# One address residue modulo 512 bytes for the operands of the split products

## The chip, the cores and the metric

The kernel runs on one core of one Trainium2 chip. The metric is the device time of one execution in microseconds. Inputs, weights and the output lie in the chip's memory, and everything is float32.

The engines are named as the profile names them: PE is TensorE's matrix multiplication, PEld its load of the stationary operand, DVE is VectorE, ACT is ScalarE, POOL is GpSimd, SP is SyncE, which issues most transfers.

## The reference

One encoder block over 1024 tokens of width 1024: a normalisation, one wide input projection, three mixers side by side (dilated window attention, grouped attention with normalised queries and keys, cross attention into 256 memory tokens), a gate on each, a projection of each, a merge by sigmoid gates, an output projection and a residual.

```python
h = rms_norm(x, g_pre[layer])
a_qkv, bq, bk, bv, mq, ga, gb, gm, mg = jnp.split(h @ w_in[layer], split_at, axis=-1)
...
ya = (oa * jax.nn.silu(ga)) @ w_br_a[layer]
yb = (ob * jax.nn.silu(gb)) @ w_br_b[layer]
ym = (om * jax.nn.silu(gm)) @ w_br_m[layer]
gates = jax.nn.sigmoid((mg + b_merge[layer]).astype(jnp.float32)).astype(dt).reshape(b, s, N_BRANCHES, d)
merged = gates[:, :, 0] * ya + gates[:, :, 1] * yb + gates[:, :, 2] * ym
out = merged @ w_out[layer]
x = x + rms_norm(out, g_post[layer])
```

## The kernel before

**Split products.** PE multiplies in a reduced format, `float32r`. To keep the precision of float32, an operand is split into a high part, rounded by a copy on ACT, and a low part, the rest, by a subtraction on DVE (`split`, lines 89 to 91). A product is then three matmuls into one PSUM bank: high by high, high by low and low by high. Each matmul loads its stationary operand (128 by 128, so 512 bytes of each partition) and streams its moving operand, 512 columns (2048 bytes of each partition) or 256 columns. In a row of the profile such as `s<-hh,vS` the first name behind the arrow is the moving operand, the second the stationary one.

**Stages**, by the line of their matmuls, in order of time:

- L354: keys and values of the grouped attention, 256 columns moving (`wbh`, `wbl`), stationary the tokens `hh`, `hl` (the split of the normalised input, eight tiles each, for the whole kernel).
- L525: keys and values of the memory, 256 columns, moving `mh`, `ml`, stationary `wh`, `wl`.
- L284, L286, L288: queries of the grouped attention, 256 columns, moving `wbh`, `wbl`, stationary `hh`, `hl`; woven with it the memory attention, whose products are L110 (`passes`), 256 columns, with `kmh`, `kml`, `mqh`, `mql`, `vmh`, `vml`, `mph`, `mpl`.
- L128, L130, L132 (`dense`): gate units, 512 columns, moving `hh`, `hl`, stationary `wh`, `wl`; woven with the grouped attention: L772 (row minima), L790 and L791 (scores), L806 (values, in float32).
- L1221 and L1272: values of the dilated attention by seven products of blocks (Strassen's scheme), 512 and 256 columns, stationary the tokens (`hh`, `hl`, and sums of tokens in `aq`, `ak`, `kT`, `vA`), moving the weights (`wh`, `wl`, `sl`).
- L1311 (`pair_product`): queries, keys, one gate and the merge gates, 25 pairs of units, again by seven products of blocks, 2100 matmuls of 512 columns. The stationary operand is a block of weights, in `wh`, `wl` or in the tiles `vS10` to `vS21`; the moving one a block of tokens, in `hh`, `hl`, `aq`, `ak`, or in `vA` and `kT` tiles.
- L1899: the merge projections, 512 columns, moving `hh`, `hl` or `bh`, `bl`, woven with the dilated attention (L1570, L1584, L1618, L1640, L1650, L1660, all float32).
- L2041: the last merge projections. L2123: the output projection by seven products of blocks, moving `wB`, `wT` tiles, stationary `hh`, `hl`, `aq`, `ak`, `wh`, `wl`.

**What sets the order.** PE's instructions stand in the order in which the program writes them; in some stages the other engines' do too, and a scheduler places the rest. Tiles come from pools. Pools on the left of the partition's memory are stacked from low addresses upward, pools on the right from the top downward, and a pool's tiles lie one behind the other, so each tile's address follows from the sizes of all that were laid before it. The left stack begins with the constants (`cs`, then `ones`, `mhalf`, `rb`, `rcol`, `nrcol`, `rsq`, `hbm`, each rounded up to 32 bytes), followed by `hh` and `hl`, the weight tiles `wr`, `wh`, `wl`, and the pools of each stage. `cs` is the table of constants that one transfer brings: 426 columns, of which 128 and 129 are unused, and 146 to 169 hold the biases of the merge gates. `ones` is a column of ones, and `hbm` half of those biases.

Of the kernel before, what the change touches and what calls it, by code (L numbers as in the profile page):

```python
# [8 lines left out]
F32 = mybir.dt.float32  # L9
R = mybir.dt.float32r  # L10
AF = mybir.ActivationFunctionType
OP = mybir.AluOpType
# [5 lines left out]
P = 128  # L18
# [4 lines left out]
C_ID, C_GP, C_GM, C_BM, C_END = 0, 130, 138, 146, 426  # L23
# [10 lines left out]
def block(ctx: ExitStack, tc: tile.TileContext, x, xT, memT, cst, msk, bcst, tabA, gpost,  # L34
          wu, wv, wb, wmem, wbr, wout, out):
    nc = tc.nc
    V, A, G, PE = nc.vector, nc.scalar, nc.gpsimd, nc.tensor

    const = ctx.enter_context(tc.tile_pool(name="const", bufs=1))
# [23 lines left out]
    def pss1():  # L63
        return bank["p"].tile([P, 512], F32, name="s1", tag="s1", bufs=bank["n"][1])

    def pst():
        bank["i"] += 1
        return bank["p"].tile([P, 4, 128], F32, name="tr", tag="t", bufs=bank["n"][2])

    def pso():  # L70
        return bank["p"].tile([P, 512], F32, name="ov", tag="o", bufs=bank["n"][3])
# [3 lines left out]
    cs = const.tile([P, C_END], F32, name="cs")  # L75
    nc.sync.dma_start(cs, cst)
    ident = cs[:, C_ID:C_ID + 128]
    ones = const.tile([P, 1], F32, name="ones")
    V.memset(ones, 1.0)
    mhalf = const.tile([P, 16], F32, name="mhalf")  # L80
    V.memset(mhalf, -0.5)
# [1 line left out]
    rcol = const.tile([P, NT], F32, name="rcol")  # L83
    nrcol = const.tile([P, NT], F32, name="nrcol")
    rsq = const.tile([P, NT], F32, name="rsq")
    hbm = const.tile([P, 24], F32, name="hbm")
    V.tensor_scalar(hbm, cs[:, C_BM:C_BM + 24], 0.5, None, op0=OP.mult)

    def split(dst_h, dst_l, src):
        A.activation(dst_h, src, AF.Copy)  # L90
        V.tensor_tensor(dst_l, src, dst_h.bitcast(F32), op=OP.subtract)  # L91
# [15 lines left out]
    def passes(out_ps, terms):  # L107
        n = len(terms)
        for i, (a, b) in enumerate(terms):
            PE.matmul(out_ps, a, b, start=i == 0, stop=i == n - 1)  # L110
# [107 lines left out]
    def pool(name, side="left"):  # L218
        p = tc.tile_pool(name=name, bufs=1, side=side, reuse_waits="tile")
        return p, p.__enter__()  # L220
# [7 lines left out]
    mbp, mb = pool("mb", "right")  # L228
# [37 lines left out]
    def fetch_wb(c0):  # L266
        raws = []
        for i in range(2):
            raw = wp.tile([P, 1024], F32, name="wr", bufs=WR)
            raws.append(raw.rearrange("p (k f) -> p k f", k=4))  # L270
        return raws, mb.tile([P, 8, 256], R, name="wbh"), mb.tile([P, 8, 256], R, name="wbl")
# [162 lines left out]

    PROJ = 8 * 24 * 109.0
    raws, *wkv = fetch_wb(512)

    def load_wkv(i):
        nc.sync.dma_start(raws[i // 2][:, i % 2 * 2:i % 2 * 2 + 2], wb[:, 2 * i:2 * i + 2, 512:768])
# [114 lines left out]
    mtp, mt_ = pool("mt")  # L554
    fp["p"] = mt_

    def m_att(h):
        qh, ql = MQ[h]
        for _ in range(4):
            yield 250  # L560
        st = {}

        def scores(n):
            sv = pss1().rearrange("p (t k) -> p t k", t=2)
            nm = mt_.tile([P, 2], F32, name="mnm", bufs=3)
            l = mt_.tile([P, 2], F32, name="mls", bufs=3)
            pm = mt_.tile([P, 2, 256], F32, name="pm", bufs=2)
            for j in range(2):
                t = slice((2 * n + j) * 128, (2 * n + j) * 128 + 128)
                passes(sv[:, j], [(qh[:, t], kmh[:, h]), (qh[:, t], kml[:, h]), (ql[:, t], kmh[:, h])])  # L570
            V.tensor_reduce(nm, sv, axis=AX.X, op=OP.min)
            V.tensor_tensor(nm, nm, rcol[:, 2 * n:2 * n + 2], op=OP.mult)
            for j in range(2):
                A.activation(pm[:, j], sv[:, j], AF.Exp, scale=nrcol[:, 2 * n + j:2 * n + j + 1], bias=nm[:, j:j + 1],
                             accum_out=l[:, j:j + 1])
            rl = mt_.tile([P, 2], F32, name="mrl", bufs=4)
            V.reciprocal(rl, l)
            for j in range(2):
                fp["mv"] = V.tensor_scalar(pm[:, j], pm[:, j], rl[:, j:j + 1], None, op0=OP.mult)
            st[n] = pm  # L580

        def trans(n):
            pm = st[n]
            tp = pst().rearrange("p (k t) q -> p k t q", k=2)
            for kt in range(2):
                for j in range(2):
                    PE.transpose(tp[:, kt, j, :], pm[:, j, kt * 128:kt * 128 + 128], ident)
            ph = mt_.tile([P, 2, 256], R, name="mph", bufs=2)
            pl = mt_.tile([P, 2, 256], R, name="mpl", bufs=2)
            split(ph, pl, tp.rearrange("p k t q -> p k (t q)"))  # L590
            st[n] = (ph, pl)

        def pv(n):
            ph, pl = st.pop(n)
            o = pso()
            terms = []
            for kt in range(2):
                terms += [(vmh[:, kt, h], ph[:, kt]), (vmh[:, kt, h], pl[:, kt]), (vml[:, kt, h], ph[:, kt])]
            passes(o[:, 0:256], terms)
            om = mt_.tile([P, 256], F32, name="om", bufs=2)  # L600
            A.activation(om, o[:, 0:256], AF.Copy)
            nc.sync.dma_start(od[2, h, :, n * 256:n * 256 + 256], om)

        for n in range(7):
            if n < 4:
                scores(n)
            yield 654
            if 0 <= n - 2 < 4:
                trans(n - 2)
            yield 436  # L610
            if 0 <= n - 3 < 4:
                pv(n - 3)
            yield 654
# [46 lines left out]
    early[len(queue)] = lambda: load_w(wu[U_G + 11])  # L660
    weave(1)
    weave(2, m_att(0), M_COST, 1.2)
    weave(2, m_att(1), M_COST, 1.2)
    weave(1, m_att(2), M_COST, 1.0)
    weave(1, m_att(3), M_COST, 1.0)
    while pend:
# [813 lines left out]
    with ExitStack():  # L1480
# [224 lines left out]
        def plan(it, pre, nxt):  # L1705
# [7 lines left out]
            def tokens(T):  # L1713
# [11 lines left out]
                if n == 11:  # L1725
                    if T == 6:
                        DL["g"] = cb.tile([P, S], F32, name="wgt", bufs=2)
                        nc.sync.dma_start(DL["g"], g2d[0, 3])
                    if T in (2, 3):
# [61 lines left out]
        def combine(p_, ogs):  # L1791
# [46 lines left out]
            def gate():  # L1838
                G.tensor_tensor(ogs[0], ogs[0], c["g"], op=OP.mult)
                DL[p_] = ogs[0]  # L1840

# [14 lines left out]

        bop, bo = pool("bo", "right")
        OPER[1] = [[bo.tile([P, S], R, name=f"b{x}{k}") for k in range(4)] for x in "hl"]
        DL = {}

        def b_load(k):
# [10 lines left out]
        def dl_load(k):  # L1872
            nc.sync.dma_start(hl[k].bitcast(F32), od[0, k])
            DL[k] = hl[k].bitcast(F32)

        def dl_high(k, t=slice(0, S)):
            A.activation(hh[k][:, t], DL[k][:, t], AF.Copy)

        def dl_low(k, t=slice(0, S)):
            G.tensor_tensor(hl[k][:, t], DL[k][:, t], hh[k][:, t].bitcast(F32), op=OP.subtract)  # L1880

# [476 lines left out]
```

## Time and profile before

| what | value |
|---|---|
| median of three runs | 1377.12 us (1377.1 to 1378.94) |
| the profiled execution, device time | 1377.47 us |
| its span, first to last instruction | 1375.7 us |
| granted clock of PE, mean | 0.999 |
| matmuls, by the profile | 8303 |

A row of a group reads: line, engine, operation, output and inputs, shape, count, then busy time in us, the mean of one in ns, and the idle time ahead of the group. Matmuls overlap: one starts before the one ahead has drained. Their starts are recorded, and their ends are modelled. So the time that a stream of them takes is read from the distance between starts, and two groups' mean durations can be compared with each other.

### The profile page before, as it was taken

How to read it: one execution, taken by the hardware profiler on the slowest of the kernel's cores; microseconds unless marked ns; L12 is line 12 of the kernel's file. 1: busy time of each engine (PE TensorE's matmuls, PEld its weight loads, DVE VectorE, ACT ScalarE, POOL GpSimd, SP SyncE). 2: the span in 40 equal slices, each digit the busy share in tenths (PEclk: the TensorE clock that was granted, in tenths of full speed). 3: DMA queues.
4: the chain of work that ended last, by engine and by line, in shares of the span. 5: the costliest groups of instructions: out<-in, count | busy, mean ns of one | idle time of the engine just before them, and what ended most of it. 6: DMA issues, size and time to landing. Idle time of an engine off the chain costs nothing.

```text
span 1375.7 us, 22888 instructions
## 1 busy us (share of the span) xinstructions
PE 1355.3 (99%) x8303; PEld 1089.5 (79%) x8303; DVE 1011.9 (74%) x1836; ACT 655.2 (48%) x1388; POOL 580.3 (42%) x443
## 2 busy tenths in 40 slices
PE   7999999999999999999999999999999999999997
PEld 7899986666666789988888888888888777778886
DVE  7868677776777498766777776687777666768977
ACT  6544365656655345323333343333335676753332
POOL 0516702676676100254455454465552134662003
PEclk9999999999999999999999999999999999999999
DMA  6356522322244678514233333332337778986445
GB/s 251 108 169 233 182 104 89 104 82 87 74 139 141 212 241 257 176 62 137 84 116 108 120 110 123 115 100 91 102 122 252 235 215 237 269 229 226 149 184 184
DMA packets 125489, 213.81 MB, mean 155 GB/s; under 512 B 32480, under 2 KB 64576, under 8 KB 125376
## 3 DMA queue, kind: packets, MB, share of 16 engines
q1 hardware_dynamic: 116064, 198.42, 44.9%
q10 hardware_dynamic: 9312, 13.93, 2.8%
q8 instruction: 65, 1.06, 0.3%
q14 instruction: 48, 0.39, 0.1%
HBM read 145.92 MB, written 66.38 MB: 154 GB/s over the span
## 4 chain that ended last, share of the span: by engine, by line
PE 91%; DVE 3%; ACT 2%; POOL 1%; issue 1%; DMA 1%; SPq 0%; DVEq 0%; POOLq 0%; ACTq 0%
PE s L1311 35%; PE d L1899 6%; PE s L1221 4%; PE s L2123 4%; PE ov L806 3%; PE sc L2041 3%; PE d L130 3%; PE d L128 3%; PE d L132 3%; PE s L1272 3%; PE s L1584 2%; PE tr L772 2%; PE s L791 2%; PE s L790 2%; PE d L525 2%; PE d L2123 2%
## 5 line engine op out<-in xcount | busy, mean ns | idle before, releaser
L797 POOL TENSOR_TENSOR bl<-bl,bp 128x512 f32<-128x512 f32 x96 | 133.0, 1385 | 54.1 <-ACT bp L793 48.6
L1311 PE MATMUL s<-hh,vS 128*128 128x512 f32 x400 | 133.4, 395 | 0.0
L1311 PE MATMUL s<-vA,vS 128*128 128x512 f32 x450 | 106.6, 390 | 0.0
L91 DVE TENSOR_TENSOR vS<-vot,vS 128x512 fp32r<-128x512 f32 x75 | 86.1, 1149 | 19.9 <-ACT vS L90 19.9
L1311 PEld LDWEIGHTS s<-vA,vS 128*128 128x128 f32 x450 | 84.5, 188 | 18.3
L793 ACT ACTIVATE bp<-s 128x512 f32<-128x512 f32 x128 | 75.7, 596 | 43.9 <-PE s L791 42.9
L773 DVE TENSOR_REDUCE bn<-tr 128x1 f32<-128x512 f32 x128 | 84.9, 683 | 13.7 <-PE tr L772 12.6
L132 PE MATMUL d<-hh,wl 128*128 128x512 f32 x224 | 89.4, 399 | 0.0
L1311 PEld LDWEIGHTS s<-hh,vS 128*128 128x128 f32 x400 | 75.3, 188 | 17.7
L128 PE MATMUL d<-hh,wh 128*128 128x512 f32 x224 | 89.1, 398 | 0.0
L130 PE MATMUL d<-hl,wh 128*128 128x512 f32 x224 | 89.0, 397 | 0.0
L1311 PE MATMUL s<-hl,vS 128*128 128x512 f32 x200 | 79.1, 395 | 0.0
L1596 ACT ACTIVATE pra<-pra,sts 128x192 f32<-128x192 f32 (+1 forms) x176 | 72.4, 415 | 13.3 <-DVE sts L1595 12.9
L1311 PE MATMUL s<-hh,wh 128*128 128x512 f32 x200 | 78.4, 392 | 0.0
L1311 PE MATMUL s<-hh,wl 128*128 128x512 f32 x200 | 78.4, 392 | 0.0
L1311 PE MATMUL s<-hl,wh 128*128 128x512 f32 x200 | 77.8, 389 | 0.0
L1595 DVE CUSTOM_DVE_ANT_0 pra<-s,mask 128x192 f32<-128x192 f32 (+1 forms) x192 | 48.9, 309 | 34.0 <-PE s L1584 20.0
L1315 ACT ACTIVATE vv<-s 128x512 f32<-128x512 f32 x50 | 29.9, 599 | 85.9 <-PE s L1311 59.2
L1055 POOL TENSOR_TENSOR vot<-wr 128x512 f32<-128x512 f32 x13 | 22.2, 1704 | 111.8 <-DVE wl L91 111.8
L806 PE MATMUL ov<-bp,VS 128*64 128x512 f32 x256 | 58.5, 599 | 0.0
L1055 POOL TENSOR_TENSOR vot<-vot,vA 128x512 f32<-128x512 f32 x12 | 19.3, 1609 | 90.7 <-DVE vS L91 90.7
L128 PEld LDWEIGHTS d<-hh,wh 128*128 128x128 f32 x224 | 42.2, 188 | 13.3 <-issue 5.5
(626 smaller groups left out, 4006.5 us busy)
## 6 DMA issues: line engine op xcount, KB each, us to landing
wr<-in_wu SPq DMA_DIRECT2D x40, 512.0 KB
vA<-in_wu SPq DMA_DIRECT2D x24, 512.0 KB
qkd<-ko SPq DMA_DIRECT2D x96, 128.0 KB
wl<-thd SPq DMA_DIRECT2D x24, 512.0 KB
wos<-os SPq DMA_DIRECT2D x12, 512.0 KB
wr<-in_wbr SPq DMA_DIRECT2D x24, 256.0 KB
aq<-qkd SPq DMA_DIRECT2D x12, 512.0 KB
ak<-qkd SPq DMA_DIRECT2D x12, 512.0 KB
```

Of the source, the lines that this page charges most:

```text
L91: V.tensor_tensor(dst_l, src, dst_h.bitcast(F32), op=OP.subtract)
L128: PE.matmul(dst, wh[:, k, :], hh[k][:, t], start=k == 0, stop=False)
L130: PE.matmul(dst, wh[:, k, :], hl[k][:, t], start=False, stop=False)
L132: PE.matmul(dst, wl[:, k, :], hh[k][:, t], start=False, stop=k == 7)
L773: fp["last"] = V.tensor_reduce(st[i]["n"][:, j, c:c + 1], s, axis=AX.X, op=OP.min)
L793: A.activation(pp, s, AF.Exp, scale=-1.0)
L797: G.tensor_tensor(lsum[i % 2], lsum[i % 2], pp, op=OP.add)
L806: PE.matmul(o[e * 64:e * 64 + 64], VS[:, kt, kv], d.pop(kt), start=kt < 2, stop=kt >= NT - 2)
L1311: PE.matmul(BANK[n, c], a, b, start=k == 0 and q == 0 and not more, stop=k == 3 and q == 2, skip_group_check=c in "XW")
L1596: A.activation(src, src, AF.Exp, scale=-1.0, bias=bias, accum_out=sts[:, 1, h, T:T + 1])
L1899: PE.matmul(ps_, a, b, start=k == 0 and q == 0, stop=k == 3 and q == 2)
L2123: PE.matmul(dst[:, e[0]:e[1]], a, b, start=k == 0 and q == 0, stop=k == 3 and q == 2)
```

## The change

No instruction is added or removed, and no loop, shape or order on PE changes. `ones` becomes column 128 of `cs`, and `hbm` is written over the biases in `cs`. That takes two small tiles out of the left stack. Three unused tiles are laid: 112 columns of float32 behind `wbh` and `wbl`, 48 behind `mqh` and `mql`, 16 behind `bh` and `bl`.

```diff
-    ones = const.tile([P, 1], F32, name="ones")
+    ones = cs[:, 128:129]
     V.memset(ones, 1.0)
...
-    hbm = const.tile([P, 24], F32, name="hbm")
-    V.tensor_scalar(hbm, cs[:, C_BM:C_BM + 24], 0.5, None, op0=OP.mult)
+    hbm = cs[:, C_BM:C_BM + 24]
+    V.tensor_scalar(hbm, hbm, 0.5, None, op0=OP.mult)
...
     raws, *wkv = fetch_wb(512)
+    mb.tile([P, 112], F32, name="pad")
...
         qh, ql = MQ[h]
+        if h == 0:
+            mt_.tile([P, 48], F32, name="pad")
...
         OPER[1] = [[bo.tile([P, S], R, name=f"b{x}{k}") for k in range(4)] for x in "hl"]
+        bo.tile([P, 16], F32, name="pad")
```

What it does to the addresses, as the two built programs have them (the address in the partition, modulo 512 bytes):

| tiles | before | with the change |
|---|---|---|
| `hh`, `hl`, `wh`, `wl`, `sl`, `aq`, `ak`, `mh`, `ml`, `mqh`, `mql`, `QH`, `QL`, `KB`, `wB` | 96 | 480 |
| `vA`, `vS`, `kT`, `wT`, `KS`, `VS`, `kmh`, `kml`, `vmh`, `vml` | 480 | 480 |
| `wbh`, `wbl`, `mph`, `mpl` | 416 | 480 |
| `bh`, `bl` | 32 | 480 |
| float32 operands: `bp` | 256 | 128 |
| float32 operands: `pra`, `app` | 448 | 320 |
| `cs`, whose first 128 columns are the identity for transposes | 128 | 128 |

Blocks inside these tiles begin at multiples of 512 bytes.

The one place where an engine's order differs is the head of DVE's program, ahead of the first `split`. Before:

```order
L79 MEMSET ones 128x1
L81 MEMSET mhalf 128x16
L87 TENSOR_SCALAR hbm<-cs 128x24 [waits DMAHW0_49]
L91 TENSOR_TENSOR wbl<-wr,wbh 128x512 [waits DMAHW1_49,Activation_49]
L256 SCALAR_TENSOR_TENSOR hl_94<-xk_132,cs,hh_86 128x512 [waits DMAHW2_49,Activation_49]
```

With the change:

```order
L81 MEMSET mhalf 128x16
L79 MEMSET cs 128x1 [waits DMAHW0_49]
L87 TENSOR_SCALAR cs<-cs 128x24
L91 TENSOR_TENSOR wbl<-wr,wbh 128x512 [waits DMAHW1_49,Activation_49]
L256 SCALAR_TENSOR_TENSOR hl_92<-xk_130,cs,hh_84 128x512 [waits DMAHW2_49,Activation_49]
```

The fill of `ones` now writes into `cs`, so it stands behind the transfer that brings `cs` (DMAHW0), where the scaling of the biases stood already. Everywhere else the instructions of every engine and what each waits for are the same in both programs.

## The prediction

> **What bounds the kernel now.** First the page: the span, the engines' busy time, the chain that ended last.
>
> ```profile
> span 1375.7 us, 22888 instructions
> PE 1355.3 (99%) x8303; PEld 1089.5 (79%) x8303; DVE 1011.9 (74%) x1836; ACT 655.2 (48%) x1388; POOL 580.3 (42%) x443
> PE 91%; DVE 3%; ACT 2%; POOL 1%; issue 1%; DMA 1%; SPq 0%; DVEq 0%; POOLq 0%; ACTq 0%
> ```
>
> PE is busy 99% of the span and carries 91% of the chain. Then the list of PE's waits, to see whether faster matmuls would only wait longer:
>
> ```profile
> PE s L354 <- ACT hh L255: 6.7, 1, 6.7
> ```
>
> This one, at start-up, is nearly all of it. Then the view by stretches, columns: stretch, its length, PE's busy time with its matmuls (the other engines follow); the second row is all of L1311.
>
> ```profile
> 100.00:200.00 100.00, 100.00 (x702) 92.87 (x701) 72.63 (x177) 47.73 (x115) 51.53 (x76) 1.00 0.49 169
> 572.50:1055.50 483.00, 483.00 (x2101) 394.75 (x2100) 353.68 (x383) 178.16 (x282) 244.86 (x146) 1.00 0.37 116
> ```
>
> PE never stands in either, and DVE, the next busiest, has 353.68 of 483.00 us. So PE's own pace sets the time there: a nanosecond on each of 2100 matmuls is 2.1 us of the span.
>
> **What equal residues are worth at 512 columns.** The question is whether today's rows already show both cases. They do. In the list of groups by shape (last columns: busy us, mean ns | idle us), L1311 has moving tiles at 96 with stationary `vS` at 480 (first four rows), both at 480 (`vA`, `kT`), and both at 96 (last three):
>
> ```profile
> L1311 PE MATMUL s<-hh,vS 128*128 128x512 f32 x400 | 133.4, 395 | 0.0
> L1311 PE MATMUL s<-hl,vS 128*128 128x512 f32 x200 | 79.1, 395 | 0.0
> L1311 PE MATMUL s<-aq,vS 128*128 128x512 f32 x150 | 43.0, 395 | 0.0
> L1311 PE MATMUL s<-ak,vS 128*128 128x512 f32 x150 | 43.0, 395 | 0.0
> L1311 PE MATMUL s<-vA,vS 128*128 128x512 f32 x450 | 106.6, 390 | 0.0
> L1311 PE MATMUL s<-kT,vS 128*128 128x512 f32 x150 | 38.2, 390 | 0.0
> L1311 PE MATMUL s<-hh,wh 128*128 128x512 f32 x200 | 78.4, 392 | 0.0
> L1311 PE MATMUL s<-hh,wl 128*128 128x512 f32 x200 | 78.4, 392 | 0.0
> L1311 PE MATMUL s<-hl,wh 128*128 128x512 f32 x200 | 77.8, 389 | 0.0
> ```
>
> Unequal 395, equal 389 to 392. Ends are modelled, so I check it by starts, in the timeline of L1221 (start, length, count):
>
> ```profile
> 482.87 2.88 PE L1221 MATMUL s<-sl,aq 128*128 128x512 f32 x12
> ...
> 488.31 1.52 PE L1221 MATMUL s<-wh,wl 128*128 128x512 f32 x6
> ...
> 493.75 1.56 PE L1221 MATMUL s<-sl,kT 128*128 128x512 f32 x6
> ...
> 499.34 0.39 PE L1221 MATMUL s<-wh,hh 128*128 128x512 f32 x1
> ```
>
> Both at 96: 24 matmuls from 482.87 to 488.31, 226.7 ns each. `sl` at 96 with `kT` at 480: 24 from 493.75 to 499.34, 232.9 ns. The same again in L2123, where `wT` (480) and `wB` (96) meet stationary tiles at 96:
>
> ```profile
> 1323.43 0.86 PE L2123 MATMUL s<-wT,wh 128*128 128x512 f32 x3
> ...
> 1334.63 0.86 PE L2123 MATMUL d<-wB,aq 128*128 128x512 f32 x3
> ...
> 1336.00 0.84 PE L2123 MATMUL d<-wB,aq 128*128 128x512 f32 x3
> ...
> 1344.84 0.84 PE L2123 MATMUL s<-wB,ak 128*128 128x512 f32 x3
> ```
>
> `wT`: 48 in 11.20 us, 233.3 ns; `wB`: 39 in 8.84 us, 226.7 ns. Three lines with different tiles agree on 5 to 6.6 ns. With the change all of them are at 480, which is what `vA,vS` is today.
>
> The terms, each its matmuls by its difference:
> - L1311: the four unequal groups are 900 matmuls, by 395 - 390 = 5 ns: 4.5 us. Some 72 more, each the last of a product whose successor's stationary block has the other residue, sit in the other rows: 0.4 us. Together 4.9 (4.0 if 392 rather than 389 or 390 is reached in places, 5.4 at 6 ns for 900).
> - L1221: 24 in the rows above and 48 with `vA`: 72 by 6.2 ns, 0.45 us.
> - L2123: the 24 `wT,wh` and 24 `wT,wl`, and 84 `wT,hl` of 512 columns: 132 by 6.6 ns, 0.87 us.
> - L1899: `bh`, `bl` at 32 beside `wh` at 96. By line (duration min/median/max):
>
> ```profile
> L1899 PE MATMUL d<-hh,wh x128: 387/395/501, 1055.8 to 1152.0; 128*128 128x512 f32 x128
> L1899 PE MATMUL d<-bh,wh x128: 390/397/504, 1152.2 to 1246.4; 128*128 128x512 f32 x128
> ```
>
> 2 to 3 ns on 192: 0.5 us.
> - Grouped attention, L772 and L790, whose one operand `KS` is at 480 and the other at 96. Neighbours from `dense`, all at 96, are slow here too:
>
> ```profile
> L790 PE MATMUL s<-QH,KS 128*128 128x512 f32 x128 | 51.8, 405 | 0.2
> L772 PE MATMUL tr<-KS,QH 128*128 128x512 f32 x128 | 51.2, 400 | 1.0 <-DVE bn L773 0.5 <-DVE QL L704 0.3
> L128 PE MATMUL d<-hh,wh 128*128 128x512 f32 x224 | 89.1, 398 | 0.0
> ```
>
> At 398 with equal residues, something else paces this stage. Bounds: 0, or 256 by 5 ns, 1.3 us; I take 0.5, nearer the low end because of that third row.
>
> Gain: 4.9 + 0.45 + 0.87 + 0.5 + 0.5 = 7.2 us.
>
> **What equal residues cost at 256 columns.** Here the rows go the other way:
>
> ```profile
> L1272 PE MATMUL s<-wh,hh 128*128 128x256 f32 x64 | 18.1, 283 | 0.0
> L525 PE MATMUL d<-ml,wh 128*128 128x256 f32 x64 | 18.1, 283 | 0.0
> L284 PE MATMUL s<-wbh,hh 128*128 128x256 f32 x64 | 17.8, 279 | 0.0
> L286 PE MATMUL s<-wbh,hl 128*128 128x256 f32 x64 | 18.0, 281 | 0.0
> L354 PE MATMUL ov<-wbh,hl 128*128 128x256 f32 x16 | 4.5, 279 | 0.0
> L110 PE MATMUL s<-kmh,mqh 128*128 128x256 f32 x32 | 9.0, 281 | 0.0
> L1272 PE MATMUL s<-wh,vA 128*128 128x256 f32 x48 | 8.6, 281 | 0.0
> ```
>
> Equal (first two, all at 96) 283; unequal 279 to 281. By line, the load of the stationary operand shows it too:
>
> ```profile
> L1272 PEld LDWEIGHTS s<-wh,hh x64: 188/192/192, 532.1 to 572.0; 128*128 128x128 f32 x64
> L1272 PEld LDWEIGHTS s<-wh,vA x48: 187/188/192, 549.5 to 566.4; 128*128 128x128 f32 x48
> ```
>
> 192 ns where the residues are equal, 188 where not. With the change every 256-column product has equal residues, so I expect 283 everywhere: L284 and L288, 256 by 4 ns, and L286, 128 by 2 ns, 1.3 us; L354, 192 by 3 ns (its first dozen are paced by the start-up), 0.55 us; L110, 192 by 2 ns, 0.4 us; L1272, 96 by 2 ns, 0.2 us. Loss 2.4 us, and on the path, since PE stands nowhere in the stretch from 100 to 200 us. If the 283 has another cause, the loss is 0; with all of these 864 at 4 ns it is 3.5 us.
>
> **What should cost nothing.** The fill of `ones` now stands behind the transfer of `cs` on DVE:
>
> ```profile
> 0.79 0.06 DVE L79 MEMSET ones<- 128x1 f32 x1 [0.79 <-PEq L2347]
> 4.79 0.69 DVE L91 TENSOR_TENSOR wbl<-wr,wbh 128x512 fp32r<-128x512 f32 x1 [1.26 <-ACT wbh L90]
> ```
>
> The next on DVE waits 1.26 us for ACT anyway and hides the 0.06; without that cover they would cost 0.06 us. The float32 products change their distances too. The largest, by line:
>
> ```profile
> L806 PE MATMUL ov<-bp,VS x256: 592/592/644, 236.3 to 451.5; 128*64 128x512 f32 x128
> ```
>
> `bp` at 256 meets blocks of `VS` at 480 and at 224, two distances, and median and minimum are one number. So I take 0, bounded by 256 at 5 ns, 1.3 us either way. Operands of DVE, ACT and POOL move as well; the stretch of L1311 above leaves DVE 129 us of room.
>
> **Sum.** 7.2 - 2.4 = 4.8 us. The span goes from 1375.7 to 1370.9 us. The profiled execution (1377.47 us, 1.8 more than its span) lies 0.35 us above the median of the runs, so from the median: 1377.12 - 4.8 = 1372.3 us. Bounds: gains from 5.6 (L1311 at 4.0, L1899 at 0.3, grouped attention at 0) to 8.6 (5.4 and 1.3 there), loss from 3.5 to 0, float32 1.3 either way. The ends together give 1376.3 and 1367.2 us.
>
> **Rivals.**
>
> *The 256-column loss does not come* (chance 0.13). The 192 ns of the loads in L1272 and L525 would be due to something that those stages share, not to the residue. For it: L286 and the `kmh` row have 281, nearly as much, with unequal residues. Against it: inside L1272 the rows change from 283 to 281 as soon as the stationary tile is `vA`. Time 1377.12 - 7.2 = 1369.9 us.
>
> *The residue does not matter* (0.12). All unequal pairs of 512 columns join a tile of the left stack with one of the right, so the 5 ns could belong to the sides, or to who wrote the tile last. Then nothing changes: 1377.1 us. Against it: `wB` tiles and `hh`, far apart in the left stack, run at 226.7 ns, and `bh` beside `wh`, 64 bytes off, only 2 to 3 ns slower than `hh`. The Trainium skill, page "SBUF — State Buffer", section "Who interferes with whom", speaks for this rival: it gives PE two independent read ports, one for the moving operand and one for the load of weights, and states that "PE and ACT never wait on anyone". By that rule the distance of two addresses costs nothing, and the time stays as it is. The 226.7 and 232.9 ns of L1221, the same engine microseconds apart with PE waiting for nothing, do not agree with it.
>
> *Everything on one residue collides* (0.04, slower). With ACT and DVE writing their high and low parts at 480 while PE reads at 480, L1311 would run as L128 does beside the grouped attention: 398 ns at equal residues. L1311's mean is now 392.4 (its nine rows, weighted by count), so 5.6 ns by 2100, 11.8 us lost, no gain there, and the rest (7.2 - 4.9 - 2.4) about 0: 1389 us. It decides from the point where L1311's mean lies above today's 392.4. Against it: `vA,vS` has that state today, with `vS` written at 480 all along, and shows 390.
>
> That the change does not do what it says is no rival: in the built program all split products but the six of `spread` (L1973) have both operands at 480.
>
> **How the numbers follow.** Forecast 0.71, the three rivals 0.13, 0.12, 0.04. Least difference that a measurement of this kernel tells from none: 0.2%, 2.75 us. The forecast's own range is 1369.9 to 1374.6 us; with its low end and the first rival together, and a part of the way to no change, the range for 8 in 10 is 1368.8 to 1375.6 us. Faster: 0.13 and nearly all of 0.71, 0.81. The same: 0.12 and 0.03 of the forecast, 0.15. Slower: 0.04.
>
> **What would show it.** In the groups of the changed kernel: `hh,vS`, `hl,vS`, `aq,vS` and `ak,vS` in L1311 at 389 to 391 instead of 395; the `kT` rows of L1221 and the `wT` rows of L2123 at starts 0.68 us apart for three, not 0.70; L1899's `bh` row like its `hh` row. L284 to L288 and L354 at 283, their loads of weights at 192. L1311's stretch some 4.9 us shorter, the one from L284 to L288 about 1.5 longer. PE's list of waits stays under 10 us: if it grows by more than a microsecond, an engine behind PE has become the limit and the forecast falls with it. It is wrong if the four L1311 groups stay at 395, or if `vA,vS`, whose addresses do not change, moves away from 390.

## The result, and the profile after

| what | before | with the change |
|---|---|---|
| median of six runs each | 1378.19 us (1377.1 to 1379.56) | 1372.6 us (1370.94 to 1374.47) |
| ratio, with its 95% interval | | 0.9961 (0.9948 to 0.9974) |
| profiled execution, device time | 1377.47 us | 1370.94 us |
| its span | 1375.7 us | 1369.1 us |

The kernel is 0.39% faster, by 5.6 us between the medians (3.6 to 7.2 by the interval). The profiled execution of the changed kernel is the fastest of its six, so its span shows 1 us more gain than the medians do. The line numbers have moved a little: L1311 is now L1314, L1272 is L1275, L1221 is L1224, L1899 is L1903, L2123 is L2127.

The page of the changed kernel, first the span, the busy time of the engines and the chain that ended last:

```profile
span 1369.1 us, 22888 instructions
PE 1349.7 (99%) x8303; PEld 1091.0 (80%) x8303; DVE 1018.1 (74%) x1836; ACT 655.5 (48%) x1388; POOL 579.8 (42%) x443
...
PE 92%; DVE 2%; POOL 2%; ACT 1%; issue 1%; DMA 1%; SPq 0%; DVEq 0%; POOLq 0%; ACTq 0%
```

PE is still the bound, and still busy 99% of the span. Its list of waits (what waited for what, us in total, times, longest) begins as before, with the start-up:

```profile
PE s L354 <- ACT hh L255: 6.6, 1, 6.6
PE s L1941 <- DVE acc L1377: 0.9, 1, 0.9
```

All its rows add up to 10.9 us, those of before to 11.9, so the waits did not grow: no engine behind PE became the limit. Then the groups by shape (last columns: busy us, mean ns, idle us):

```profile
L1314 PE MATMUL s<-hh,vS 128*128 128x512 f32 x400 | 131.1, 389 | 0.0
L1314 PE MATMUL s<-vA,vS 128*128 128x512 f32 x450 | 106.1, 389 | 0.0
...
L1314 PE MATMUL s<-hh,wl 128*128 128x512 f32 x200 | 78.1, 391 | 0.0
...
L1314 PE MATMUL s<-hh,wh 128*128 128x512 f32 x200 | 77.8, 389 | 0.0
L1314 PE MATMUL s<-hl,vS 128*128 128x512 f32 x200 | 77.8, 389 | 0.0
...
L1314 PE MATMUL s<-aq,vS 128*128 128x512 f32 x150 | 42.1, 389 | 0.0
L1314 PE MATMUL s<-ak,vS 128*128 128x512 f32 x150 | 42.1, 389 | 0.0
```

The four groups that stood at 395 are at 389. So are two rows whose residues had been equal all along: `hh,wh` was at 392, `vA,vS` at 390. The stretch from the first matmul of this line to the first of the next stage, of the kernel before and then of the changed one (length, PE, PEld, DVE, ACT, POOL):

```profile
572.48:1055.82 483.34, 483.34 (x2102) 395.02 (x2101) 354.02 (x383) 178.50 (x282) 244.86 (x146) 1.00 0.37 116
```

```profile
574.75:1051.18 476.43, 476.43 (x2103) 393.96 (x2102) 358.73 (x383) 179.15 (x282) 244.30 (x146) 1.00 0.37 118
```

2100 matmuls take 6.91 us less, with the same work beside them. The timeline of L1224 and L2127 (start, length, count) shows the other two rows that were to move:

```profile
496.03 1.52 PE L1224 MATMUL s<-sl,kT 128*128 128x512 f32 x6
...
501.47 0.39 PE L1224 MATMUL s<-wh,hh 128*128 128x512 f32 x1
...
1317.43 0.84 PE L2127 MATMUL s<-wT,wh 128*128 128x512 f32 x3
...
1328.31 0.84 PE L2127 MATMUL d<-wB,aq 128*128 128x512 f32 x3
```

`sl,kT`: 24 starts in 5.44 us, 226.7 ns each (before 232.9). `wT`: 48 in 10.88 us, 226.7 ns (before 233.3).

At 256 columns the rows went up, as forecast. By line for L1275 (duration min/median/max) and by group:

```profile
L1275 PEld LDWEIGHTS s<-wh,vA x48: 192/192/192, 551.6 to 568.6; 128*128 128x128 f32 x48
L1275 PE MATMUL s<-wh,vA x48: 283/283/283, 551.7 to 568.7; 128*128 128x256 f32 x48
```

```profile
L288 PE MATMUL s<-wbl,hh 128*128 128x256 f32 x64 | 18.1, 283 | 0.0
...
L284 PE MATMUL s<-wbh,hh 128*128 128x256 f32 x64 | 18.1, 282 | 0.0
```

The load of `wh,vA` went from 188 to 192 ns, the matmul from 281 to 283. To see where the time went, the span is cut at the first matmul of each stage. Each number is a stage's length in the profiled execution, less the same stage before (us; "again" is a second profile of the same changed kernel, the last experiment below):

| stage (line numbers of before) | before | with the change | again |
|---|---|---|---|
| L354 | 25.81 | +0.75 | +0.91 |
| L284 to L288, with L110 | 69.00 | +1.61 | +1.73 |
| rest of L110, to L772 | 52.56 | +0.11 | +0.11 |
| grouped attention | 241.78 | -0.06 | +0.18 |
| L1221 | 76.67 | -0.19 | +0.19 |
| L1272 | 40.17 | +0.14 | +0.14 |
| L1311 | 483.34 | -6.91 | -6.95 |
| L1899 | 190.84 | -0.97 | -1.13 |
| L2123 to the end | 85.20 | -0.86 | -0.85 |

Rows left out are all within 0.1 us, but for the wait at start-up. The gain is L1311 and L2123, 7.8 us. The stages of the 256-column products take back 2.6 (L354, L284 to L288, L110, L1272). That leaves 5.2 us, next to 5.6 between the medians.

Only a part of L354's 0.75 us is the pace of its stream. Its starts lie 120.0 ns apart instead of 117.5, which is 0.43 us for the 170 matmuls behind the start-up. Ahead of them, at the start of the program, matmuls come some 213 ns apart: 13 of them in the profile before, 20 with the change, 22 in the second profile. The seven more are worth 0.7 us; a gap of 0.45 us late in the stage, ahead of L242, is 0.12 with the change and gives 0.33 back. The number of slow matmuls at the start goes from 14 to 24 in the versions below, and it is 21 in the one that has the old distances again, so it is not put down to the addresses. By pace alone the loss is 2.3 us.

### The profile page after: what moved, and what is told of

The parts are those of the page before. It is cut to its first block, busy times and chain, and to the rows that moved or that the text cites. A ratio compares the mean times of both kernels' runs of the same rounds, so it can differ in the third digit from the quotient of the medians.

```text
span 1369.1 us, 22888 instructions
## 1 busy us (share of the span) xinstructions
PE 1349.7 (99%) x8303; PEld 1091.0 (80%) x8303; DVE 1018.1 (74%) x1836; ACT 655.5 (48%) x1388; POOL 579.8 (42%) x443
## 4 chain that ended last, share of the span: by engine, by line
PE 92%; DVE 2%; POOL 2%; ACT 1%; issue 1%; DMA 1%; SPq 0%; DVEq 0%; POOLq 0%; ACTq 0%
PE s L1314 35%; PE d L1903 6%; PE s L1224 4%; PE s L2127 4%; PE ov L809 3%; PE sc L2045 3%; PE d L130 3%; PE d L128 3%; PE d L132 3%; PE s L1275 3%; PE s L1587 2%; PE tr L775 2%; PE s L794 2%; PE s L793 2%; PE d L526 2%; PE d L2127 2%
## 5 line engine op out<-in xcount | busy, mean ns | idle before, releaser
L1314 PE MATMUL s<-hh,vS 128*128 128x512 f32 x400 | 131.1, 389 | 0.0
L1314 PE MATMUL s<-vA,vS 128*128 128x512 f32 x450 | 106.1, 389 | 0.0
L91 DVE TENSOR_TENSOR vS<-vot,vS 128x512 fp32r<-128x512 f32 x75 | 89.4, 1192 | 19.9 <-ACT vS L90 19.9
L1314 PEld LDWEIGHTS s<-vA,vS 128*128 128x128 f32 x450 | 84.5, 188 | 17.5
L1314 PEld LDWEIGHTS s<-hh,vS 128*128 128x128 f32 x400 | 75.1, 188 | 15.6
L1314 PE MATMUL s<-hh,wl 128*128 128x512 f32 x200 | 78.1, 391 | 0.0
L1314 PE MATMUL s<-hl,wh 128*128 128x512 f32 x200 | 77.9, 389 | 0.0
L1314 PE MATMUL s<-hh,wh 128*128 128x512 f32 x200 | 77.8, 389 | 0.0
L1314 PE MATMUL s<-hl,vS 128*128 128x512 f32 x200 | 77.8, 389 | 0.0
```

What stands on the lines that cost most here:

```text
L1314: PE.matmul(BANK[n, c], a, b, start=k == 0 and q == 0 and not more, stop=k == 3 and q == 2, skip_group_check=c in "XW")
```

## The experiments

Three questions stood open. Does the distance of the two addresses set the pace, or something that L1311's operands share in another way (which side of memory, who wrote them last)? Is 512 bytes the period? And can the 256-column products be given a better distance than zero?

### PE alone, one distance after the other

One tile `ST` and one tile `MV`, written once by ACT. Then streams of matmuls, one line of code for each distance; only the start inside `MV` differs, by a distance in bytes (0, 32, 64 and so on up to 480, and 16, 512 and 768). A few more lines start both operands at 96, 256 and 480. One of the lines, for a distance of 128 bytes, which is 32 columns:

```diff
+    for i in range(36): PE.matmul(bk[i // 12 % 4][:, :512], ST[:, 0 + 128 * (i % 8):0 + 128 * (i % 8) + 128], MV[:, 32 + 512 * (i % 3):32 + 512 * (i % 3) + 512], start=i % 12 == 0, stop=i % 12 == 11)  # N512 d128 base0
```

> Leaves out the whole block: PE alone multiplies blocks of two tiles, one line of the program for each distance (address of the moving operand minus address of the stationary one, modulo 512 bytes), 36 matmuls of 512 columns or 48 of 256 or 128 columns a line, with no other engine at work. Theory (the distance of the two operands sets the pace of a stream, at 512 columns equal residues are the fast case, at 256 columns the slow one): 512 columns at distance 0, 512 and whatever the common residue (96, 256, 480) about 227 ns from start to start, at 128 and 384 about 233, at 448 about 230 to 233; 256 columns at distance 0 about 120 ns, at 128 and 384 about 118.6, at 320 and 448 about 116.5. Distance 768 like 256, and 256 not like 0 if the period is 512 bytes. Rival (the pools' sides, or the tile that another engine wrote last, set the pace): one number at every distance, for each width, since all blocks lie in the same two tiles and nothing writes them meanwhile. Rival (only a collision with the writes of other engines costs): also one number, near 224 for 512 columns.

Measured, the groups by shape at distances 128, 384, 256 and 0 with 512 columns, then 0, 128 and 16 with 256 columns:

```profile
L40 PE MATMUL bk<-MV,ST 128*128 128x512 f32 x36 | 8.6, 395 | 0.0
L48 PE MATMUL bk<-MV,ST 128*128 128x512 f32 x36 | 8.6, 395 | 0.0
...
L44 PE MATMUL bk<-MV,ST 128*128 128x512 f32 x36 | 8.3, 390 | 0.0
...
L36 PE MATMUL bk<-MV,ST 128*128 128x512 f32 x36 | 8.3, 389 | 0.0
...
L58 PE MATMUL bk<-MV,ST 128*128 128x256 f32 x48 | 5.9, 283 | 0.0
...
L62 PE MATMUL bk<-MV,ST 128*128 128x256 f32 x48 | 5.9, 282 | 0.0
...
L74 PE MATMUL bk<-MV,ST 128*128 128x256 f32 x48 | 5.6, 276 | 0.0
```

L36 and L44 (distances 0 and 256) are fast, L40 and L48 (128 and 384) slow. The view by stretches shows that nothing else ran, for most of the program (length, PE, PEld, ACT, POOL; DVE has no instruction in it):

```profile
60.00:400.00 340.00, 340.00 (x2323) 313.16 (x2323) 0.00 (x0) 0.00 (x0) 1.00 0.00 1
```

Mean distance between starts, ns:

| distance, bytes | 0 | 16 | 32 | 64 | 96 | 128 | 160 | 192 | 224 | 256 | 320 | 384 | 512 | 768 |
|---|---|---|---|---|---|---|---|---|---|---|---|---|---|---|
| 512 columns | 226.7 | 231.7 | 233.4 | 229.1 | 233.7 | 233.4 | 234.3 | 233.3 | 233.2 | 227.3 | 229.1 | 233.4 | 227.3 | 226.7 |
| 256 columns | 119.7 | 113.3 | 117.9 | 117.9 | 119.8 | 118.6 | 118.7 | 117.8 | 118.3 | 119.9 | | | 119.9 | |

At 128 columns every distance gives 111.6 or 111.7, but for the first line, distance 0, with 110.5 (111.6 in its second half). So the two addresses alone do it, between two tiles that one engine wrote, with no other engine at work. The sides of memory, the last writer and a collision with other engines' writes are not needed. The period is 256 bytes, not 512. And at 256 columns a distance of 16 is much better than any other here. Two values that the expectation had taken from the kernel missed: 256 columns at 320 and 448 ran at 117.9 and 117.8, not 116.5.

A mean holds the first matmuls of its stream too. The last line of the program, 512 columns at distance 0 once more, behind the streams of 128 columns, has 229.6 over all and 226.6 in its second half.

### The change at another multiple of 256, and 128 bytes away

The changed kernel with an unused tile ahead of the constants, which moves the left stack against the right one: 256 bytes in the first, 128 in the second (`[P, 32]`).

```diff
+    const.tile([P, 64], F32, name="pad")
     cs = const.tile([P, C_END], F32, name="cs")
```

> The changed kernel with 256 bytes more at the bottom of the left stack: the left tiles at 224, the right ones still at 480, so nothing that joins the two sides is equal modulo 512, and everything is equal modulo 256. Theory by the first experiment (the period is 256 bytes): the same time as the changed kernel, 1372.6 us, L1311 at 389. Rival (the period is 512, as the change has it): the gain of the change is gone, L1311's groups with vS as the stationary tile at 395, 1378 us.

> The changed kernel with 128 bytes more at the bottom of the left stack: left tiles at 96, right tiles at 480, distances of 128 or 384 as before, with the two tiles still in the table and the pads still there. Theory: the gain at 512 columns goes (L1311 with vS 395, L1221 with kT, L2123 with wT 233 ns a start), L284 to L288 and L354 at 281 to 282; 1377.5 to 1378.5 us, as the kernel before. Rival (moving the two tiles into the table brought the gain, by what waits for them): 1372.6 us as the changed kernel.

Measured: 1371.88 us for 256 bytes (1369.52 to 1374.36), ratio to before 0.9957 (0.9944 to 0.997). And 1378.84 us for 128 bytes (1377.36 to 1379.79), ratio 1.0007 (0.9998 to 1.0016). Groups of the second, L1311 now L1315:

```profile
L1315 PE MATMUL s<-hh,vS 128*128 128x512 f32 x400 | 133.4, 395 | 0.0
L1315 PE MATMUL s<-vA,vS 128*128 128x512 f32 x450 | 106.6, 390 | 0.0
...
L1315 PE MATMUL s<-hh,wh 128*128 128x512 f32 x200 | 78.5, 392 | 0.0
```

And its stretch of L1315:

```profile
574.32:1057.66 483.34, 483.34 (x2102) 395.25 (x2101) 354.12 (x383) 178.40 (x282) 244.90 (x146) 1.00 0.36 116
```

With the two tiles still inside the table and the pads in place, 128 bytes of padding bring back 483.34 us, the number of the kernel before to two decimals. At 256 bytes it is 476.42. So L1311's gain is the distance of the addresses and nothing else in the change. The 392 of `hh,wh` came back too, though both its operands are at 96. Expected were 1372.6 us for the first and 1377.5 to 1378.5 for the second.

### Without the three pads

```diff
-    mb.tile([P, 112], F32, name="pad")
...
-        if h == 0:
-            mt_.tile([P, 48], F32, name="pad")
...
-        bo.tile([P, 16], F32, name="pad")
```

> The changed kernel without its three pads: the two tiles alone stay moved. The left stack is at 480 as in the change, wbh and wbl at 416, mph and mpl at 288, bh and bl at 32. Theory (512 columns gain at equal residues, 256 columns lose): L1311, L1221 and L2123 keep their whole gain; L284 to L288 and L354 keep the 279 to 281 of before instead of 283, some 1.4 us less than the changed kernel; L1899 keeps 397 for bh beside wh, 0.4 us more: 1371.6 us, 0.9993 of the changed kernel, 0.9954 of the kernel before. Rival (every product is better at equal residues): slower than the changed kernel by 1 to 3 us, 1374 us.

Measured: 1370.13 us (1368.55 to 1372.77), ratio to before 0.9944 (0.9929 to 0.9958). The stretch of L1311 is 476.44 us. The group of L284, and the list of PE's waits:

```profile
L284 PE MATMUL d<-wbh,hh 128*128 128x256 f32 x64 | 17.7, 277 | 0.0
```

```profile
PE s L110 <- ACT pm L574: 0.6, 1, 0.6
```

The pads bring nothing that shows; by the stages they cost. Without them L354 is as long as before (-0.07 instead of +0.75) and L284 to L288 only 0.30 longer. The expectation had the pace there as before, and that missed: PE is faster than before (277 against 279). From start to start it is 113.4 ns in L354 (117.5 before, 120.0 with the change) and 114.2 to 114.8 in L284 to L288 (116.5 and 119.7; means by line, without the gaps above 140 ns). The addresses agree: without its pad `wbh` is at 416 and `hh` at 480, a distance of 192 modulo 256, and PE alone ran 256 columns at 113.7 there in the next experiment, though at 117.8 in the first. So the pads keep these products from a distance that is fast in this kernel. The time did not follow all the way: L354 has 19 slow matmuls at the start instead of 13, and PE stands 0.6 us for ACT in L110, which it didn't. The interval overlaps that of the change, so the 2.3 us between the two ratios rest on the stages: L354, L284 to L288 and the rest of L110 are 2.3 us shorter than with the change (0.82, 1.31 and 0.13).

### Finer distances, PE alone

As the first, with distances in steps of 4 bytes up to 64, other starts for both operands, and float32 products.

> Leaves out the whole block, as in e1: PE alone, one line for each distance, now in steps of 4 bytes from 0 to 60, of 16 bytes from 64 to 240, then blocks whose common residue is 4, 8 or 16, both operands 16 bytes off, and distances of -16 and -64, for 512 and for 256 columns; at the end five lines of float32 products (512 columns, 64 wide) at distances 0, 16, 32, 64 and 128. Theory (the distance modulo 256 sets the pace): a smooth set of values by distance, 512 columns slowest away from 0 (231 to 234), a drop towards 229 at 64; 256 columns 113 at 16, and at the other distances that are odd multiples of 16, 118 to 120 at multiples of 32; the common residue changes nothing, -16 is as good as 16. Rival (the alignment of the moving operand's own address to 32 bytes is what gave 113 at 16): both operands 16 bytes off give 113 as well, and all distances that are no multiple of 32 give it. Float32: the same duration at all five distances.

Measured, 512 columns at distance 4, at 16, and both operands 4 bytes off at distance 0 (L71); then distance 0:

```profile
L44 PE MATMUL bk<-MV,ST 128*128 128x512 f32 x36 | 8.7, 400 | 0.0
L71 PE MATMUL bk<-MV,ST 128*128 128x512 f32 x36 | 8.7, 399 | 0.0
...
L47 PE MATMUL bk<-MV,ST 128*128 128x512 f32 x36 | 8.5, 394 | 0.0
...
L43 PE MATMUL bk<-MV,ST 128*128 128x512 f32 x36 | 8.3, 389 | 0.0
```

Mean distance between starts, ns:

| distance | 0 | 4 | 8 | 12 | 16 | 20 | 28 | 64 | 112 | 192 | 240 | 0, both 4 off | 0, both 16 off |
|---|---|---|---|---|---|---|---|---|---|---|---|---|---|
| 512 columns | 226.7 | 237.9 | 233.1 | 229.4 | 231.8 | 233.8 | 229.6 | 229.2 | 231.1 | | 226.9 | 237.7 | 231.1 |
| 256 columns | 119.9 | 122.9 | 117.0 | 116.7 | 113.3 | 122.1 | 115.6 | 117.8 | 113.3 | 113.7 | 117.1 | 122.3 | 116.8 |

Float32 products take 429.1 to 431.4 ns for each of their passes at distances 0 to 128: no effect. So "equal residues" is not the whole rule. Equal at 4 or 16 bytes is slow, and 240 is as fast as 0. The expectation missed in three points: the common residue does matter; at 256 columns the other odd multiples of 16 are not fast (119.9 at 80, 118.3 at 48; only 112 is); and -16 is not as good as 16 (117.3). Its rival, the 32-byte alignment of the moving operand, fell as well, since both operands 16 bytes off give 116.8. At 256 columns a distance of 192 gave 113.7 here and 117.8 in the first experiment, with the same starts inside the two tiles. So the distance alone does not fix the pace: at least at this one there are two. What sets it stays open.

### A distance of 16, then of 112, for the 256-column products

The moving operands of 256 columns, but for the last 24 products (in L2123), begin 16 bytes behind the common residue, by tiles that are 256 bytes longer and used from column 4 on. In the second it is 112 bytes (from column 28 on). The 512-column products keep distance 0 modulo 256.

```diff
-        return raws, mb.tile([P, 8, 256], R, name="wbh"), mb.tile([P, 8, 256], R, name="wbl")
+        return raws, *[mb.tile([P, 2112], R, name=z)[:, 4:2052].rearrange("p (k f) -> p k f", k=8) for z in ("wbh", "wbl")]
...
-        h, l = wslot(0), wslot(1)
+        h, l = [wp.tile([P, 1088], R, name=z)[:, 4:1028] for z in ("wh", "wl")]
```

> The changed kernel with the moving operand of every 256-column product but the last 24 laid 16 bytes behind the common residue (wbh, wbl, mh, ml, kmh, kml, mph, mpl, and the weights of L1272, each in a tile 256 bytes longer), the 512-column products left at equal residues. Theory (a stream's pace is set by the two operands' places alone, so what PE did alone in the first two experiments holds in the kernel): 256 columns at 113.3 ns from start to start instead of 120, rows of 276 instead of 283: L284 to L288 384 by 6.5, L354 192 by 6.5, L525 192 by 6.5, L110 192 by 6, L1272 336 by 6.6 ns, together 8.6 us less than the changed kernel: 1364 us, 0.990 of the kernel before; L1272's stretch 38.1 us instead of 40.3. Rival (113 is a pattern into which only PE alone settles; other operands and other engines' traffic break it): 117 to 118 ns, 3 us less, 1369.5 us, 0.994.

> As e6, with 112 bytes in place of 16, the other distance at which 256 columns ran at 113.3 ns with PE alone. Theory: the same 1364 us and the same rows of 276. Rival (only the smallest distance works, because the two addresses then lie in one stretch of 32 bytes): 1369 us or more, rows of 279 to 283.

Measured: 16 bytes, 1369.84 us (1367.9 to 1371.26), ratio to before 0.9942 (0.9929 to 0.9954). 112 bytes, 1368.65 us (1366.54 to 1370.87), ratio 0.9935 (0.9921 to 0.9948): the lowest ratio of all versions, though its interval overlaps those of 16 bytes and of the version without pads. Both expectations had 1364 us. The same group of L1272 (here L1269) with 16 and then with 112 bytes; with the change it is at 283:

```profile
L1269 PE MATMUL s<-wh,hh 128*128 128x256 f32 x64 | 17.9, 280 | 0.0
```

```profile
L1269 PE MATMUL s<-wh,hh 128*128 128x256 f32 x64 | 17.6, 275 | 0.0
```

The 113.3 ns of 16 bytes did not hold in the kernel: starts lie 118.1 to 118.6 ns apart in L1269, L352 and L282 to L286 (L1272, L354 and L284 to L288 of before; means as above), and the time is what the rival gave (1369.5 us). Those of 112 bytes did hold in these lines: 113.6 to 114.4, against 119.7 to 120.0 with the change; L523 and L109 (L525 and L110 of before) came to 115.5 and 116.4. But the time followed only in part. L1272's stretch, 335 distances, should have come down by some 6.4 ns each, 2.1 us; it went from 40.31 to 39.83 (with 16 bytes it is 40.77). PE's waits with 112 bytes, in rows that are new or larger than with the change:

```profile
PE tr L1647 <- DMA avs<-vdr: 1.7, 2, 1.2
PE s L1218 <- DVE hl L91: 1.1, 1, 1.1
...
PE s L1269 <- DVE wl L91: 0.8, 1, 0.8
...
PE s L109 <- ACT pm L572: 0.5, 1, 0.5
PE s L1269 <- ACT wh L90: 0.4, 1, 0.4
```

PE now reaches products whose operands DVE and ACT are still splitting. In L1269 it stands 1.2 us, which is most of the 1.7 that are missing in that stretch. In L1218, just ahead, it stands 1.1 us, and that stage is 1.1 us longer than with the change. So there the engines behind PE have become the limit. The whole list of waits adds up to 14.5 us against 10.9 with the change; the row of L1647, which reads 0.3 to 1.4 us in the other versions, is not put down to the 112 bytes.

### The change again

The changed kernel itself, on the chip and beside the runs of the two before.

> The changed kernel itself, beside the two before it on one chip. Theory: 0.995 to 0.997 of the kernel before, L1311's stretch 476.4 us, L284 to L288 70.6 us. Rival (the 6.6 us between the two profiled spans were partly the chance of one execution): L1311's stretch off by more than 0.5 us from 476.4.

Measured: 1371.88 us (1370.61 to 1373.79), ratio to before 0.9962 (0.9949 to 0.9974). L1311's stretch is 476.39 us. On this chip the 112 bytes bring 3.2 us more than the change, and the two intervals do not overlap (up to 0.9948, and from 0.9949).

## Why the prediction was right, and where it was not

**The mechanism and the sign were right.** All operands on one residue make the 512-column products faster and the 256-column products slower, and the first weighs more: 0.39% faster measured, 0.35% forecast. That the time came to within 0.3 us owes something to luck. The difference was forecast as 4.8 us and is 5.6 between the medians; the three runs of before that the forecast began from lie 1.1 us below the six that the result is compared with, and that made up for it. The rule, one residue modulo 512 bytes, was narrower than what the experiments show: the period is 256.

**L1311 was mis-sized: 4.9 us forecast, 6.9 measured.** The step took 972 matmuls by 395 - 390 = 5 ns, from mean durations, whose ends are modelled. Sorting the starts of this line in the profile before by the residues of the pair gives its true rate (ns to the next start):

```
residues of the pair, and of the next one's stationary block      matmuls    before    with the change
unequal here or at the join                                         972      232.8         226.7
both at 96                                                          551      228.3         227.4
both at 480                                                         576      227.6         226.7
```

(With the change all pairs are equal; the rows keep their names.) Unequal pairs lost 6.1 ns, not 5: 5.9 us instead of 4.9. And the 1127 pairs that were equal all along lost 0.9 ns each where they stood among unequal ones, 1.0 us, nearly all of it in `hh,wh` (229.9 to 227.1) and `vA,vS` (227.8 to 226.7). The forecast counted that as nothing, although it had quoted `hh,wh` at 392. That it goes with the neighbours is seen in `vA,vS`, whose two addresses the change does not move, and in the shift by 128 bytes: `hh,wh`, both at 96, is at 392 there, and at 389 in every version whose other pairs are equal modulo 256. The place 96 itself is not slow, for in L1221 and L2123 pairs at 96 ran at 226.7 before. The starts that the prediction itself read in L1221 (226.7 and 232.9) had nearly the right difference.

**L2123: 0.87 us forecast, 0.86 measured.** Here the step used starts, not durations.

**L1221: 0.45 forecast, and the rows are as forecast** (226.7 ns), but the stage is 0.19 us shorter in one profile and 0.19 longer in the other. The timeline shows what takes it back, near the stage's end:

```profile
531.16 0.61 PE L1224 MATMUL s<-sl,hh 128*128 128x512 f32 x2
531.78 0.50 PE L1224 MATMUL s<-sl,hl 128*128 128x512 f32 x1
```

From the start of two matmuls to the start of the third it takes 0.62 us there, where two distances are 0.45, and the next comes 0.11 late as well: 0.27 us of the 0.45. In the second profile four long distances, two of them here, cost 0.65 us, and its list names a wait of 0.2 us for DVE at this product: the third matmul reads the low part that DVE has just made, and PE arrives earlier than before. With 112 bytes this same product waits 1.1 us. With 256 bytes of padding no distance of the stage is long, and there it is 0.51 us shorter than before, as the term has it.

**The loss at 256 columns: 2.4 forecast, 2.6 measured,** of which 2.3 is pace. The parts are near their terms: L354 0.75, by pace 0.43 (0.55), L284 to L288 with the L110 that is woven in and the rest of L110 1.72 (1.7 for L284 to L288 and L110), L1272 0.14 (0.2). The rows are at 282 and 283, the loads at 192. The cause that the step gave, "equal residues", is only a part of it: by the finer distances 256 columns are slow at most distances and fast at a few. One that can be fast, 192, is where L284 to L288 and L354 lie without the pads.

**L1899: 0.5 forecast, not settled.** The medians of its rows moved as forecast; by line:

```profile
L1903 PE MATMUL d<-hh,wh x128: 387/394/504, 1051.2 to 1147.2; 128*128 128x512 f32 x128
L1903 PE MATMUL d<-bh,wh x128: 387/395/504, 1147.4 to 1240.8; 128*128 128x512 f32 x128
```

`bh` was at 397 and is at 395, `hh` at 394. But the stage, woven with the dilated attention, is 1.0 and 1.1 us shorter in the two profiles of the change, and 0.3 longer with 256 bytes of padding, where the residues are as equal. Over the profiles of all versions it goes from 189.3 to 191.3 us, and 0.5 can't be seen in that. PE alone bears the size out: a distance of 64 bytes, as `bh` had, costs 229.1 - 226.7 = 2.4 ns, and 192 of these are 0.46 us.

**Grouped attention: 0.5 forecast, nothing measured** (-0.06 and +0.18 of 241.78 us). The row that argued for the low end, neighbours at equal residues at 398, was the one to follow to the end, to a term of 0.

**The float32 products: 0 forecast.** PE alone shows no effect of the distance on them (429.1 to 431.4 ns a pass).

**Two readings of the prediction were wrong,** though the sum does not rest on them. The wait at start-up, 6.7 us, is not nearly all of PE's list of waits: the list adds up to 11.9 us. So the sign "stays under 10 us" was broken before the change; what counts is that it did not grow (10.9). And the sign that speaks against the forecast if `vA,vS` moves away from 390 came, by 1 ns: it took a row's time to depend on its own addresses alone, and the neighbours count too.

**The rivals.** "The 256-column loss does not come" fell: the loads and rows are where they were forecast. "Everything on one residue collides" fell: every L1314 group is at 389 to 391. "The residue does not matter" fell twice, with PE alone and with 128 bytes of padding. The Trainium skill, page "SBUF — State Buffer", section "Who interferes with whom", which spoke for it, says that PE never waits on anyone. Whether another engine's accesses hold PE up was not tried, and so that may stand. But taken as a statement that it has no price where PE's own two operands lie, it does not agree with 226.7 against 233.4 ns with every other engine at rest.

## What to carry to other kernels

Where one engine's steady stream fills the span, read its pace from the starts of its instructions, group by group, and compare groups that differ in one thing; a difference of 6 ns in 230 was worth 7 us here. Padding that puts two operands at the same place modulo some number is free to try, but try it for each shape by itself: what helped 512 columns hurt 256, and the pads that made everything equal kept two stages from a faster distance. The neighbours of a slow group may be slow with it, and belong in the sum.

## What was not expected of the hardware

- The period is 256 bytes: 227.3 ns at a distance of 256, 226.7 at 0 and 768, 233.4 at 128 and 384 (512 columns, PE alone).
- Equal residues were fast at starts that are multiples of 32 bytes (226.7 to 228.0 at 0, 96, 256 and 480), but 231.1 with both operands at 16 and 237.7 with both at 4. And they are not the only fast case: 226.9 with the stationary operand at 0 and the moving one at 240, 226.7 with 16 and 32.
- At 256 columns the pace goes from 113.3 (distances 16 and 112) through 119.9 (0) to 122.9 (4). For one distance it can be 113.7 or 117.8, and the 113.3 of 16 bytes became 118.1 to 118.6 in the kernel.
- At 128 columns (111.6 to 111.7 ns once a stream is under way) and for float32 (429.1 to 431.4 ns a pass) the distance makes no difference.
- Matmuls whose own addresses do not change can gain when their neighbours' do: `vA,vS` in L1311 went from 227.8 to 226.7 ns.
